# A two-layer decoder trunk on one core: pads in SBUF that move matmul operands to other offsets modulo 256 bytes, and the inverse norm spread by transposes in place of products

## The chip, the cores and the metric

The kernel runs on one core of one Trainium2 chip, in one launch. The metric is the device time of that core in microseconds, from runs of the whole kernel. TensorE (PE; its weight loads are shown apart, as PEld), VectorE (DVE), ScalarE (ACT), GpSimd (POOL) and SyncE (SP, which here only issues DMAs) are separate engines that meet at semaphores. Each of them works through its own instructions in the order in which they stand in the program.

## The reference

Two layers on a sequence of 256 positions with 1024 features, all in float32. Layer 0 mixes tokens with a gated linear recurrence (RG-LRU), layer 1 with sparse attention in three branches. A squared-ReLU MLP follows each, with an RMS norm ahead of every part and one at the end.

```python
def _rmsnorm(x, g):
    y = xf * lax.rsqrt(jnp.mean(xf * xf, axis=-1, keepdims=True) + RMS_EPS)
    return (y * g.astype(jnp.float32)).astype(x.dtype)

def _sq_relu_mlp(h, w_up, w_down):
    u = jax.nn.relu(h @ w_up)
    return (u * u) @ w_down

def reference(x, ...):
    for i in range(DEPTH):
        h = _rmsnorm(x, norm_mix[i])
        if i % N_MIXERS == 0:
            x = x + _rglru_mixer(h, ...)
        else:
            x = x + _nsa_mixer(h, ...)
        h = _rmsnorm(x, norm_ffn[i])
        x = x + _sq_relu_mlp(h, mlp_w_up[i], mlp_w_down[i])
    return _rmsnorm(x, norm_final)
```

`_rglru_mixer` is a projection to 2048 features, a causal convolution of width 4, two sigmoid gates from block-diagonal products, a scan over the sequence and a projection back. `_nsa_mixer` is a projection to queries, three pairs of keys and values and gates; a compressed branch whose softmax also scores blocks; a selected and a window branch; and a projection back.

## The kernel before

**Layout.** Activations lie transposed: 128 features on the partitions, 256 positions along the free axis, eight such chunks for 1024 features. Weights arrive in pieces of 128x1024 values by DMA (tile `raw`, 5 buffers). Every product of a weight piece is made in three matmuls so that it keeps float32's precision: a weight `w` is split into a rounded part `whi` (ACT, sometimes DVE) and the rest `wlo` (DVE), 7 buffers of each, and an activation into such a pair too. `mm3` (L313 to L315) then issues `whi` by the high part, `whi` by the low part, `wlo` by the high part, all into one PSUM bank. One such matmul has a stationary operand of 128x128 (a 512-byte stretch of `whi` or `wlo` in each partition), and a moving operand of 128x256 (1024 bytes in each partition).

**Moving operands.** `hhl` holds the pair of the normalised input, for the projections (`conv`, `branch`, `proj`, MLP up). `uhl` holds that of the squared ReLU, for MLP down. `xbh` and `xbl` hold that of the recurrence's output, for its output projection (`out`, 192 matmuls). `oh` and `ol` hold that of the attention's output. In attention, `kh` and `kl` are the moving operands of the scores (L1095, L1096, with the queries `sa` or `sb` stationary), `kc` that of the compressed scores (L1032), `pth` and `ptl` those of the product of probabilities and values (L1160, L1162, with `vhl` stationary), and `pc` that of the compressed branch (L1167, with `bhl` stationary). The recurrence's gates (L656) are plain float32 products with `gw` stationary and `xb` moving.

**Stages.** The recurrence, the attention and the lead into each MLP are written as tasks with due times, durations and dependencies; a planner (`Plan`) turns them into one order for each engine when the program is built. The two MLPs are plain loops: 32 up pieces and 32 down pieces each, 24 matmuls a piece. PE has work from the first pieces to the last in one stream. DVE and ACT prepare the weight pieces ahead of it.

**The norm.** The factor 1/sqrt(mean square) is applied after the projection, so the projections need not wait for it. Four times in the program (`Section.stats`) and once at its end these steps run: `square_sums` (L491) sums the squares of the features for 128 positions at a time, with a column of ones moving, which leaves the sums with the positions on the partitions; ACT takes the square root (L408) and DVE the reciprocal (L410) into `rcol`, 128x2; `spread` (L496) brings it back along the free axis, equal on all partitions; ACT copies that from PSUM to `rs`, called `rstd` in the profile (L412). DVE then multiplies projections by `rs` as it reads them from PSUM. At the end of the program the last step is left out: DVE multiplies `xg` by the PSUM bank itself (L1274) and the result goes out by DMA.

**Pools.** A pool of buffers gives each tile the next free bytes of every partition, in the order in which the tiles are named. A tile in its midst therefore sets where all the later ones of that pool start.

Of the kernel before, what the change touches and what calls it, by code (L numbers as in the profile page):

```python
# [12 lines left out]
F32 = mybir.dt.float32  # L13
# [6 lines left out]
P = 128  # L20
S = 256
# [203 lines left out]
def trunk_kernel(ctx: ExitStack, tc: tile.TileContext, x_in, vec_in, const_in, w2_in, wts, out):  # L225
    nc = tc.nc
    ctx.enter_context(tc.manual_schedule())
    pe, dve, act, pool = nc.tensor, nc.vector, nc.scalar, nc.gpsimd
# [9 lines left out]
    def bank(i):  # L238
        return psum.tile([P, 512], F32, name="bank%d" % i, tag="bank%d" % i)
# [88 lines left out]
    class Section:  # L328
# [73 lines left out]
        def stats(self, srcs, t):  # L402

            b6 = [("ps", 6)]
            st = self.bank(("stats", t), 6, lambda x: x)
            for j, (x, k) in enumerate(srcs):
                self.add("pe", 0.32, lambda e, j=j, x=x: square_sums(st(), x, j == 0, j == len(srcs) - 1), r=[k], w=b6, t=t)
            self.add("act", 0.15, lambda e: e.activation(rcol, st()[:, :2], AF.Sqrt, bias=epst, scale=1.0 / D), r=b6 + ["tab"],  # L408
                     w=["rcol"], t=t)
            self.add("dve", 0.08, lambda e: e.reciprocal(rcol, rcol), w=["rcol"], t=t)  # L410
            self.add("pe", 0.43, lambda e: spread(st()), r=["rcol", "cst"], w=b6, t=t)
            self.add("act", 0.26, lambda e: e.copy(rs, st()[:, S:]), r=b6, w=["rs"], t=t)  # L412
# [36 lines left out]
    ident = cst[:, C_ID:C_ID + P]  # L449
# [7 lines left out]
    rcol = spool.tile([P, 2], F32, name="rcol")  # L457
# [35 lines left out]
    def spread(st):  # L493

        for i in range(2):
            pe.matmul(st[:, S + i * P:S + (i + 1) * P], rcol[:, i:i + 1].to_broadcast([P, P]), ident, start=True, stop=True)  # L496

    def residual(z, m):
        dve.tensor_tensor(xt[:, m], xt[:, m], z, op=OP.add)  # L499
# [2 lines left out]
    with ExitStack() as ph:  # L502
        rg = ph.enter_context(tc.tile_pool(name="rg", bufs=1))
# [91 lines left out]
        small(lambda e: e.tensor_scalar(sp, sp, 4.0, None, op0=OP.mult), [], ["sp"])  # L595

        xb_b, r_b, i_b, y_b, t_b = (rg.tile([P, 8, S], F32, name=n) for n in ("xb", "r", "i", "y", "t"))
        xbh_b, xbl_b = (rg.tile([P, 8, S], F32R, name=n) for n in ("xbh", "xbl"))
        xb, r_t, i_t, y_t, t_t, xbh, xbl = ([x[:, m] for m in range(8)] for x in (xb_b, r_b, i_b, y_b, t_b, xbh_b, xbl_b))
        pair = lambda x, m: x[:, m // 2 * 2:m // 2 * 2 + 2]  # L600
# [185 lines left out]
    with ExitStack() as ph:  # L786
        at = ph.enter_context(tc.tile_pool(name="at", bufs=1))
# [14 lines left out]
        th, tl = many([P, S], F32R, "th", 2), many([P, S], F32R, "tl", 2)  # L802
        ptt = at.tile([P, NPT * 6 * P], F32, name="pt")
        pts = [ptt[:, i * 6 * P:(i + 1) * 6 * P] for i in range(NPT)]
        kh = at.tile([P, 4, 2 * S], F32R, name="kh")
        kl = at.tile([P, 4, 2 * S], F32R, name="kl")
        kc = at.tile([P, 4, 2, NCP], F32R, name="kc")
        osumt = at.tile([P, 2, S], F32, name="osum")
        osum = [osumt[:, i] for i in range(2)]
        identf = cst[:, C_ID:C_ID + P]  # L810
        zw = [at.tile([P, 8 * S], F32, name="zw" + n, tag=n) for n in ("oh", "ol")]
        ohl = {}

        def opart(n, i):

            if n not in ohl:
                ohl[n] = at.tile([P, 8 * S], F32R, name=n, tag=n)
            return ohl[n][:, i * S:(i + 1) * S]

        oh, ol = (lambda i, n=n: opart(n, i) for n in ("oh", "ol"))  # L820
        ptht, ptlt = (at.tile([P, NTH * 3 * P], F32R, name=n) for n in ("pth", "ptl"))
        pth, ptl = ([x[:, i * 3 * P:(i + 1) * 3 * P] for i in range(NTH)] for x in (ptht, ptlt))
        add("pool", 0.15, lambda e: e.memset(kc.bitcast(F32), 0.0), w=["kc0"], t=-9)
# [442 lines left out]
    st = bank(6)  # L1266
    mlp(1, to_final, up1, lambda: square_sums(st, acc, True, False))
    square_sums(st, sqs[1], False, True)
    act.activation(rcol, st[:, :2], AF.Sqrt, bias=epst, scale=1.0 / D)
    dve.reciprocal(rcol, rcol)  # L1270
    spread(st)

    for i, (a, n) in enumerate(((0, 1), (1, 1), (2, 2), (4, 2), (6, 1), (7, 1))):
# [113 lines left out]
```

## Time and profile before

| | us |
|---|---|
| median of 3 runs | 593.32 |
| lowest and highest run | 591.52, 593.86 |
| span of the profiled execution, first to last instruction | 588.7 |
| PE busy in that span | 572.6 |
| DVE busy | 421.5 |
| ACT busy | 356.5 |

The page gives the profiled execution by its span; a time of its own beside the span isn't given. The median of the runs lies 4.6 us above the span.

A row of the groups reads: line, engine, operation, output<-inputs, shapes, count, then the busy time in us and the mean time of one in ns, then the idle time of the engine ahead of them and what ended it. A matmul's time in such a row is from its start to its modelled end; the next one on PE starts well before that end. How fast PE goes through a row of matmuls is read from their starts, or from the number of them in a window. A plain float32 product of 128x128 operands is one instruction in the program and two records in the profile; a transpose is one.

### The profile page before, as it was taken

The page shows a single profiled execution, that of the slowest core. Times are in us where ns is not written, and L with a number is a line of the kernel's source. Part 1 is how long each engine was busy: PE and PEld are TensorE (multiplying, and loading weights), DVE is VectorE, ACT ScalarE, POOL GpSimd, SP SyncE. Part 2 cuts the span into 40 slices and gives each one's busy share as a digit, 9 for nine tenths or more (in the row PEclk, how much of TensorE's full clock was granted, in tenths as well). Part 3 has the DMA queues.
Part 4 walks back from the last instruction along what each step waited for, and adds up shares of the span by engine and source line. Part 5 has one row for each costly group of instructions (what it writes and reads, how often), then busy time and mean ns, then how long its engine had stood idle before and what let it go on. Part 6 is the DMA issues. An engine that isn't in the chain of part 4 may idle for free.

```text
span 588.7 us, 12309 instructions
## 1 busy us (share of the span) xinstructions
PE 572.6 (97%) x4798; PEld 559.1 (95%) x4798; DVE 421.5 (72%) x862; ACT 356.5 (61%) x711; POOL 75.2 (13%) x110
## 2 busy tenths in 40 slices
PE   7999999999999999999999999989999999999994
PEld 7999999999999999999989997879999999999994
DVE  6899997776766546547679999989876776464522
ACT  7699583766664325336367999996866564343410
POOL 2210000000001113125211532000000000132320
PEclk9999999999999999999999999999999999999998
DMA  8934665665666665657954641143776667466302
GB/s 285 386 119 136 208 221 183 216 206 183 192 201 197 210 205 175 210 188 228 232 197 144 180 128 52 37 125 99 238 201 199 188 206 239 158 183 228 126 2 72
DMA packets 32682, 105.74 MB, mean 180 GB/s; under 512 B 4832, under 2 KB 6496, under 8 KB 32624
## 3 DMA queue, kind: packets, MB, share of 16 engines
q1 hardware_dynamic: 30224, 100.70, 53.3%
q0 software_dynamic: 1824, 3.72, 2.5%
q8 instruction: 38, 0.62, 0.5%
q10 hardware_dynamic: 576, 0.53, 0.3%
q14 instruction: 20, 0.16, 0.1%
HBM read 99.23 MB, written 1.05 MB: 170 GB/s over the span
## 4 chain that ended last, share of the span: by engine, by line
PE 81%; ACT 8%; DVE 6%; issue 3%; DMA 1%; POOL 0%; SPq 0%; DVEq 0%; ACTq 0%; POOLq 0%
PE bank L315 25%; PE bank L313 25%; PE bank L314 25%; PE bank L656 2%; ACT pt L1105 2%; ACT pt L1124 2%; DVE wlo L318 1%; ACT pth L1138 1%; ACT whi L321 1%; PE bank L906 1%; DMA raw<-in_dram 1%; ACT osum L1171 1%; DVE ptl L1139 1%; DVE pt L1102 1%; DVE osum L1174 1%
## 5 line engine op out<-in xcount | busy, mean ns | idle before, releaser
L313 PE MATMUL bank<-hhl,whi 128*128 128x256 f32 x768 | 214.3, 279 | 1.6 <-DVE whi L321 1.6
L315 PE MATMUL bank<-hhl,wlo 128*128 128x256 f32 x768 | 212.7, 277 | 0.8 <-DVE wlo L318 0.8
L314 PE MATMUL bank<-hhl,whi 128*128 128x256 f32 x768 | 212.3, 276 | 0.0
L282 DVE TENSOR_TENSOR wlo<-raw,whi 128x1024 fp32r<-128x1024 f32 x118 | 147.3, 1269 | 2.7 <-ACT whi L273 2.7
L313 PEld LDWEIGHTS bank<-hhl,whi 128*128 128x128 f32 x768 | 144.2, 188 | 2.2 <-ACT whi L321 1.5
L315 PEld LDWEIGHTS bank<-hhl,wlo 128*128 128x128 f32 x768 | 144.2, 188 | 1.6 <-DVE wlo L318 1.4
L314 PEld LDWEIGHTS bank<-hhl,whi 128*128 128x128 f32 x768 | 144.4, 188 | 0.1
L313 PE MATMUL bank<-uhl,whi 128*128 128x256 f32 x512 | 141.4, 276 | 0.0
L315 PE MATMUL bank<-uhl,wlo 128*128 128x256 f32 x512 | 141.4, 276 | 0.0
L314 PE MATMUL bank<-uhl,whi 128*128 128x256 f32 x512 | 141.4, 276 | 0.0
L273 ACT CAST whi<-raw 128x1024 fp32r<-128x1024 f32 x119 | 120.9, 1039 | 23.7 <-issue 18.8
L314 PEld LDWEIGHTS bank<-uhl,whi 128*128 128x128 f32 x512 | 96.1, 188 | 0.0
L313 PEld LDWEIGHTS bank<-uhl,whi 128*128 128x128 f32 x512 | 96.1, 188 | 0.0
L315 PEld LDWEIGHTS bank<-uhl,wlo 128*128 128x128 f32 x512 | 96.1, 188 | 0.0
L318 DVE TENSOR_TENSOR wlo<-raw,whi 128x1024 fp32r<-128x1024 f32 (+3 forms) x72 | 76.0, 1073 | 2.6 <-ACT whi L321 2.6
L499 DVE TENSOR_TENSOR xt<-xt,bank 128x256 f32<-128x256 f32 x40 | 16.0, 417 | 85.6 <-PE bank L315 85.4
L321 ACT CAST whi<-raw 128x1024 fp32r<-128x1024 f32 (+2 forms) x65 | 61.5, 957 | 17.4 <-PE bank L314 9.5
L751 ACT ACTIVATE u<-t 128x256 f32<-128x256 f32 x64 | 26.7, 417 | 54.9 <-DVE t L746 54.9
L746 DVE SCALAR_TENSOR_TENSOR t<-bank,rstd 128x256 f32<-128x256 f32 x64 | 26.9, 423 | 42.5 <-PE bank L315 41.7
L469 POOL TENSOR_TENSOR acc<-xt 128x256 f32<-128x256 f32 x2 | 3.0, 1522 | 301.1 <-DVE xt L499 301.1
L1264 ACT ACTIVATE xg<-xt,vec 128x256 f32<-128x256 f32 x8 | 4.1, 510 | 48.0 <-DVE xt L499 48.0
L1105 ACT ACTIVATE pt<-pt,mx 128x256 f32<-128x256 f32 (+1 forms) x64 | 28.7, 452 | 3.4 <-DVE mx L1102 3.2
(201 smaller groups left out, 830.5 us busy)
## 6 DMA issues: line engine op xcount, KB each, us to landing
raw<-in_dram SPq DMA_DIRECT2D x175, 512.0 KB, 4.3
gw<-in_dram SPq DMA_DIRECT2D x4, 512.0 KB, 8.4
raw<-in_dram SPq DMA_DIRECT2D x6, 256.0 KB, 5.3
xt<-in_dram SPq DMA_DIRECT2D x4, 256.0 KB, 5.0
kh<-th POOLq DMA_DIRECT2D x16, 64.0 KB, 4.2
raw<-in_dram SPq DMA_DIRECT2D x2, 456.0 KB, 4.8
zwoh<-in_dram SPq DMA_DIRECT2D x1, 512.0 KB, 4.9
zwol<-in_dram SPq DMA_DIRECT2D x1, 512.0 KB, 6.2
```

The costliest lines, as they stand in the source:

```text
L273: (act.copy if eng is None else eng.tensor_copy)(hi_t[i % NSPL][:, :n], raw_t[i % NRAW][:, :n])
L282: (eng or dve).tensor_tensor(lo[:, :n], raw_t[i % NRAW][:, :n], hi[:, :n].bitcast(F32), op=OP.subtract)
L313: pe.matmul(ps, wh, xh, start=start, stop=False)
L314: pe.matmul(ps, wh, xl, start=False, stop=False)
L315: pe.matmul(ps, wl, xh, start=False, stop=stop)
L318: return lambda e: e.tensor_tensor(o, a, h.bitcast(F32), op=OP.subtract)
L321: return lambda e: (e.copy if e is act else e.tensor_copy)(o, a)
L499: dve.tensor_tensor(xt[:, m], xt[:, m], z, op=OP.add)
L656: e.matmul(z(), gw[b][:, o:o + P], xb[2 * b + k], start=k == 0, stop=k == 1)
L746: dve.scalar_tensor_tensor(t, z, 0.0, rs, op0=OP.max, op1=OP.mult)
L751: act.activation(u, t, AF.Square)
L1105: add("act", (0.39, 0.49)[qc], lambda e, row=row, j=j: e.activation(row, row, AF.Exp, bias=mx[:, j:j + 1], scale=-1.0, accum_out=sm[:, j:j ...
```

## The change

Two parts. The first puts four tiles that nothing reads or writes into the pools: 128 bytes ahead of `xbh` in the recurrence, and 64, 192 and 64 bytes at three places in the attention. The second makes `spread` issue two transposes of the broadcast `rcol`, where it issued two float32 products with the identity. The stationary operand (`rcol`, one column repeated 128 times) and the moving one (the 128x128 identity in `cst`) are the same in both forms, and so is what they write.

```diff
     def spread(st):
 
         for i in range(2):
-            pe.matmul(st[:, S + i * P:S + (i + 1) * P], rcol[:, i:i + 1].to_broadcast([P, P]), ident, start=True, stop=True)
+            pe.transpose(st[:, S + i * P:S + (i + 1) * P], rcol[:, i:i + 1].to_broadcast([P, P]), ident)
...
         xb_b, r_b, i_b, y_b, t_b = (rg.tile([P, 8, S], F32, name=n) for n in ("xb", "r", "i", "y", "t"))
+        rg.tile([P, 32], F32, name="rgap")
         xbh_b, xbl_b = (rg.tile([P, 8, S], F32R, name=n) for n in ("xbh", "xbl"))
...
         pts = [ptt[:, i * 6 * P:(i + 1) * 6 * P] for i in range(NPT)]
+        at.tile([P, 16], F32, name="gap0")
         kh = at.tile([P, 4, 2 * S], F32R, name="kh")
         kl = at.tile([P, 4, 2 * S], F32R, name="kl")
         kc = at.tile([P, 4, 2, NCP], F32R, name="kc")
...
+        at.tile([P, 48], F32, name="gap1")
         zw = [at.tile([P, 8 * S], F32, name="zw" + n, tag=n) for n in ("oh", "ol")]
...
+        at.tile([P, 16], F32, name="gap2")
         ptht, ptlt = (at.tile([P, NTH * 3 * P], F32R, name=n) for n in ("pth", "ptl"))
```

Where the operands of the matmuls start within a partition, modulo 256 bytes, in the built program:

| operand | before | after |
|---|---|---|
| `whi`, `wlo` (stationary in `mm3`) | 32 | 32 |
| `hhl`, `uhl` | 224 | 224 |
| `oh`, `ol` (and `zw`, which shares their bytes) | 224 | 224 (256 bytes further on) |
| `xbh`, `xbl` | 96 | 224 |
| `gw` (stationary) | 192 | 64 |
| `xb` (moving with `gw`) | 96 | 96 |
| `kh`, `kl`, `kc` | 224 | 32 |
| `sa`, `sb`, `vhl`, `bhl` (stationary in attention) | 96 | 96 |
| `pth`, `ptl` | 224 | 32 |
| `pc` | 32 | 96 |

Tiles that only DVE, ACT or POOL work on and that are named behind a pad move too (`xp`, `a2`, `osum`, `mx`, `sm`, `cs` and others).

No engine's instructions change their order, and none is added or removed but those of `spread`, which keep their places. The planner's durations are not touched.

## The prediction

> **What bounds the kernel now.** I read the page first: engines, slices, chain.
>
> ```profile
> PE 572.6 (97%) x4798; PEld 559.1 (95%) x4798; DVE 421.5 (72%) x862; ACT 356.5 (61%) x711; POOL 75.2 (13%) x110
> PEclk9999999999999999999999999999999999999998
> PE 81%; ACT 8%; DVE 6%; issue 3%; DMA 1%; POOL 0%; SPq 0%; DVEq 0%; ACTq 0%; POOLq 0%
> ```
>
> PE is busy for 97% of the span at full granted clock, and 81% of the chain that ended last is PE's. So a nanosecond on a matmul counts, unless PE then waits for something else. A mean time from start to modelled end doesn't give the pace; starts do. I therefore asked for windows of PE alone in which one form fills the whole stretch: the recurrence's output projection, then the two MLPs.
>
> ```profile
> 66.40:88.20 21.80, 21.80 (x187) 1.00 0.72 239
> 95.70:260.00 164.30, 164.30 (x1452) 1.00 0.63 202
> 412.60:575.80 163.20, 163.20 (x1443) 1.00 0.56 176
> ```
>
> After the stretch come busy time and, in brackets, the matmuls that touch it; about two of these started before it. All are 128x128 by 128x256. In the MLPs a start follows the last one after 164.30/1450 = 113.3 ns (the second: 163.20/1441 = 113.3). In the output projection it takes 21.80/185 = 117.8 ns. The same difference stands in the groups of these windows, as 280 ns against 276:
>
> ```profile
> L314 PE MATMUL bank<-xbl,whi 128*128 128x256 f32 x62 | 17.4, 280 | 0.0
> L314 PE MATMUL bank<-uhl,whi 128*128 128x256 f32 x245 | 67.6, 276 | 0.0
> ```
>
> PE waits in neither (0.0 idle), and the stationary operands lie at 32 modulo 256 in both. What differs is the moving one: 96 for `xbl`, 224 for `uhl`. So this trace has two paces, **113.3 and 117.8 ns**, 4.5 apart, and the offset goes with them. It isn't all, though. The chain that ended last, in order of time around the third norm:
>
> ```profile
> 266.79 0.11 PE bank L313
> 266.90 0.11 PE bank L314
> 267.13 0.11 PE bank L313
> 267.54 0.58 PE bank L491 x4
> 268.12 0.23 PE bank L313
> 268.34 0.12 PE bank L314
> 268.46 0.12 PE bank L315
> 268.58 0.12 PE bank L313
> ```
>
> With `hhl` at 224 throughout, PE drops from 0.11 us a matmul to 0.12 when the square sums (L491) come between. It stays there until the spread, and returns behind it, as the timeline of the second norm shows:
>
> ```profile
> 94.57 0.28 PE L314 MATMUL bank<-hhl,whi 128*128 128x256 f32 x1
> 94.69 0.28 PE L315 MATMUL bank<-hhl,wlo 128*128 128x256 f32 x1
> 94.80 0.61 PE L496 MATMUL bank<-cst,rcol 128*128 128x128 f32 x4
> 95.17 0.37 PE L313 MATMUL bank<-hhl,whi 128*128 128x256 f32 x1
> 95.37 0.28 PE L314 MATMUL bank<-hhl,whi 128*128 128x256 f32 x1
> 95.49 0.28 PE L315 MATMUL bank<-hhl,wlo 128*128 128x256 f32 x1
> 95.60 0.28 PE L313 MATMUL bank<-hhl,whi 128*128 128x256 f32 x1
> 95.72 0.28 PE L314 MATMUL bank<-hhl,whi 128*128 128x256 f32 x1
> ```
>
> So the pace can also be held by what came just before. Behind each of the four spreads in the program it is the quick one, and behind two of them it then holds for a whole MLP.
>
> **The change, part by part.** *Output projection.* `xbh` and `xbl` go from 96 to 224, with `whi` and `wlo` at 32: the pair of the MLP rows. 192 matmuls x 4.5 ns = **0.86 us**. PE doesn't wait in that stretch, and the projection's last residual starts the norm, so the end moves with it.
>
> *Spread.* Four records become two. In the rows above they take 95.17 - 94.80 = 0.37 us to the next matmul's start. Transposes of this form run in attention:
>
> ```profile
> 327.99 0.28 PE L315 MATMUL bank<-hhl,wlo 128*128 128x256 f32 x1
> 328.11 0.49 PE L1135 MATMUL bank<-cst,pt 128*128 128x128 f32 x3
> 328.36 0.37 PE L313 MATMUL bank<-hhl,whi 128*128 128x256 f32 x1
> 328.56 0.28 PE L314 MATMUL bank<-hhl,whi 128*128 128x256 f32 x1
> ```
>
> Three take 0.25 us to the next start. The last step is about 0.03 and the others 0.11, so two take 0.14 and a spread saves 0.23. At the first, second and fourth PE goes on without a wait, so it counts: 0.69. At the third it doesn't, for PE stands at 271.2 for a weight piece that hangs on ACT and DVE, not on the spread:
>
> ```profile
> 268.89 1.06 ACT whi L321
> 269.98 1.24 DVE wlo L318
> 271.26 0.38 PE bank L315
> ```
>
> The fifth stands in the tail, where nothing hides it:
>
> ```profile
> 581.39 0.17 DVE L1270 RECIPROCAL rcol<-rcol 128x2 f32<-128x2 f32 x1 [0.99 <-ACT rcol L1269]
> 581.62 0.71 PE L496 MATMUL bank<-cst,rcol 128*128 128x128 f32 x4 [0.55 <-DVE rcol L1270]
> 582.37 0.75 DVE L1274 TENSOR_TENSOR xg<-xg,bank 128x256 f32<-128x256 f32 x2 [0.80 <-PE bank L496]
> ```
>
> It gives 0.22, two steps of 0.11. Spread in all: **0.91 us**.
>
> *Attention's operands.* `kh`, `kl`, `pth` and `ptl` go from 224 to 32 with stationary operands at 96. That is the pair that `pc` and `bhl` have now:
>
> ```profile
> L1160 PE MATMUL bank<-pth,vhl 128*128 128x256 f32 x16 | 4.5, 280 | 0.0
> L1167 PE MATMUL bank<-pc,bhl 128*128 128x256 f32 x16 | 3.2, 283 | 0.0
> L656 PE MATMUL bank<-xb,gw 128*128 128x256 f32 x64 | 14.1, 379 | 0.0
> ```
>
> Neither is at 276. Against a gain, the new pair stands at 283. For one, 224 less 32 and 32 less 96 are both 192 modulo 256, and `pc` runs only two at a time, which may not be enough to settle. Bounds for these 128 matmuls: nothing, or 128 x 4.5 = 0.58 us; the other way 128 x 3 = 0.38 lost (283 against 280). I take 0.2 gained, near the middle, since part of it lies beside waits for ACT and DVE. `pc` (16 matmuls) and `kc` (32 columns) are too few or too short to count. `gw` moves to 64: its matmuls take 379 ns for the two passes, long enough to cover a load, so I take nothing, with 64 x 4.5 = 0.29 either way. DVE's and ACT's tiles that move keep their cost: nothing in the groups of these engines separates equal shapes by offset.
>
> *Sum:* 0.86 + 0.91 + 0.2 = 1.97 us. The profiled execution would span 588.7 - 2.0 = 586.7; with the 4.6 us by which the runs' median lies above the span, **591.3 us**, 0.3% less. Neither part changes what any engine issues elsewhere, so no DMA starts for another reason, and SP's and POOL's queues are untouched.
>
> One rule speaks against the pads. The Trainium skill, "TensorE: Matmul & The Clock Gate", section "Step-by-step: what each phase is for", has TensorE read its moving and its stationary operand through two independent ports, so that the next load takes nothing from the running matmul. By that alone, offsets wouldn't matter and the sum would be the spread's 0.9 us. This trace disagrees as far as it goes: 117.8 against 113.3 ns in one form.
>
> **The rivals.** *1. Transposes leave PE in the slow pace (slower).* What sets the pace behind an interruption the views don't tell. Behind square sums it is the slow one all five times that `mm3` follows, behind the product spread the quick one all four times. Transposes are in between. Windows of the matmuls behind them, in attention:
>
> ```profile
> L314 PE MATMUL bank<-hhl,whi 128*128 128x256 f32 x5 | 1.4, 281 | 0.0
> L314 PE MATMUL bank<-hhl,whi 128*128 128x256 f32 x8 | 2.2, 277 | 0.0
> ```
>
> The first is the stretch 319.2 to 320.7, the second 328.8 to 331.0. By starts in the timeline, of 14 places where `mm3` with an operand at 224 follows transposes, 11 reach the quick pace and 3 stay slow. If the second spread ends slow, nothing in MLP 0 breaks the stretch: 1450 matmuls x 4.5 = 6.5 us. The fourth does the same to MLP 1: 1441 x 4.5 = 6.5 us. Both: 591.3 + 13.0 = **604.3**; one: 597.8. It decides as soon as a slow stretch outlasts some 440 matmuls (1.97/0.0045). For it: both spreads are entered alike, from square sums and twelve slow matmuls, so a bad entry would hit both; the three slow places show that transposes can do it. Against: 11 of 14, and of those entered at a slow pace with no wait inside, 328.11 comes out quick.
>
> *2. The offset isn't the cause.* The pace of the output projection then has another reason, the pads give nothing, and only the spread's 0.9 us is left: 592.4. Against it, the two MLPs, `oh` and `hhl` are all quick at 224, while all three operands of the projection's `mm3` are slow at 96.
>
> *3. The transposes leave the clock.* The Trainium skill, same page, section "Part 4: PE-mode transpose", says that transposes don't count as busy for the clock gate. By it PE could be throttled behind them. The granted clock in the slices above is full through attention, with its 104 transposes, so no time is put to it.
>
> **How the numbers follow.** The forecast, quick pace kept: 0.55, with its own range 590.0 to 592.6 (bounds above: 0.58 gained or 0.38 lost in attention, 0.29 for `gw`, and some tenths between executions). Both MLPs slow: 0.30, more than 3/14, since one of the slow places is, as the spreads are, entered from slow `hhl` matmuls (320.99). One MLP slow: 0.08. Pads without effect: 0.07. To leave out no more than 2 in 10 the range has to reach rival 1: **590.0 to 605.2**. About 0.5% (3 us) is what a measurement of this kernel can tell from no change. Faster by more needs 3.0 us where I find 2.0: 0.09. Within it: the rest of the forecast and rival 2, 0.53. Slower: 0.38.
>
> **What would show it.** Output projection: 276 ns in place of 280 and 113.3 by starts. Spread: two records and about 0.14 us to the next start. MLPs: windows of 1450 matmuls stay near 164.3 us; at 170.8 rival 1 holds, and `uhl` rows read 281. Attention: `pth` and `kl` rows at 276 in place of 280. I would be wrong in the mechanism if `xbl` stays at 280, and in the main risk if the pace behind a spread isn't that of the whole MLP.

## The result, and the profile after

The changed kernel takes **597.58 us**, the median of nine executions; the kernel before takes 593.32 in nine beside them. The ratio is 1.0073, with a 95% interval of 1.0044 to 1.0102: slower, where 0.3% less was forecast. (The ratios here are the record's own; where a kernel's times fall into groups some us apart, they aren't the quotient of the medians.) Seven of the nine lie between 597.2 and 599.3; one took 592.6 and one 601.1.

The page of the changed kernel, engines, clock and chain:

```profile
PE 580.2 (97%) x4788; PEld 566.8 (95%) x4788; DVE 421.8 (71%) x862; ACT 356.8 (60%) x711; POOL 74.9 (13%) x110
PEclk9999999999999999999999999999999999999998
PE 79%; ACT 9%; DVE 5%; issue 3%; DMA 2%; POOL 1%; SPq 1%; DVEq 0%; ACTq 0%; POOLq 0%
```

PE has ten records fewer and is busy 7.6 us longer, at full clock; DVE, ACT and POOL are as before. Windows of PE alone say where, as in the prediction; the first is the output projection, then MLP 0 and MLP 1:

```profile
62.50:92.00 29.50, 29.50 (x253) 1.00 0.64 210
96.50:260.00 163.50, 163.50 (x1445) 1.00 0.63 202
413.50:576.50 163.00, 163.00 (x1386) 1.00 0.56 177
```

With two matmuls off for the start, as before: 117.5 ns a start in the projection, 113.3 in MLP 0, **117.8 in MLP 1**. Two rows of the timeline tie MLP 1 down, the fourth spread and the square sums behind the MLP, in the kernel before and then in the changed one:

```profile
411.64 0.61 PE L496 MATMUL bank<-cst,rcol 128*128 128x128 f32 x4
575.99 0.50 PE L491 MATMUL bank<-ones,acc 128*128 128x1 f32 x4
```

```profile
412.62 0.38 PE L496 MATMUL bank<-cst,rcol 128*128 128x128 f32 x2
583.15 0.50 PE L491 MATMUL bank<-ones,acc 128*128 128x1 f32 x4
```

Up to the fourth spread the changed kernel is 0.98 us late (412.62 - 411.64). From there to the square sums it takes 170.53 us against 164.35, so 6.18 more. The rest takes 595.5 - 583.15 = 12.35 us against 588.7 - 575.99 = 12.71, so 0.36 less. The sum is the 6.8 us by which the span grew. Nearly all of it is what rival 1 of the prediction puts to one MLP, 6.5 us.

Groups of the changed kernel that answer to those of the prediction:

```profile
L314 PE MATMUL bank<-xbl,whi 128*128 128x256 f32 x64 | 18.0, 281 | 0.0
L1164 PE MATMUL bank<-pth,vhl 128*128 128x256 f32 x16 | 4.5, 281 | 0.0
L496 PE MATMUL bank<-cst,rcol 128*128 128x128 f32 x10 | 2.0, 277 | 0.6 <-DVE rcol L1274 0.6
```

`xbl` stays at 281, though it now stands at 224. `pth` stays too. Only the spread did what was said.

### The profile page after: what moved, and what is told of

Its sections match the earlier page's. It is cut to its first block, busy times and chain, and to the rows that moved or that the text cites. A ratio compares the mean times of both kernels' runs of the same rounds, so it can differ in the third digit from the quotient of the medians.

```text
span 595.5 us, 12289 instructions
## 1 busy us (share of the span) xinstructions
PE 580.2 (97%) x4788; PEld 566.8 (95%) x4788; DVE 421.8 (71%) x862; ACT 356.8 (60%) x711; POOL 74.9 (13%) x110
## 4 chain that ended last, share of the span: by engine, by line
PE 79%; ACT 9%; DVE 5%; issue 3%; DMA 2%; POOL 1%; SPq 1%; DVEq 0%; ACTq 0%; POOLq 0%
PE bank L313 25%; PE bank L315 25%; PE bank L314 24%; ACT pt L1109 3%; PE bank L657 2%; ACT pt L1128 2%; ACT pth L1142 1%; ACT whi L321 1%; DMA kl<-tl 1%; DVE wlo L318 1%; PE bank L910 1%; ACT osum L1175 1%; SPq L346 1%; DMA vec<-in_dram 1%; DVE osum L1178 1%
## 5 line engine op out<-in xcount | busy, mean ns | idle before, releaser
L313 PE MATMUL bank<-hhl,whi 128*128 128x256 f32 x768 | 216.5, 282 | 0.8 <-DVE whi L321 0.8
L315 PE MATMUL bank<-hhl,wlo 128*128 128x256 f32 x768 | 214.9, 280 | 0.5 <-DVE wlo L318 0.5
L314 PE MATMUL bank<-hhl,whi 128*128 128x256 f32 x768 | 214.5, 279 | 0.0
```

The source lines that it names most:

```text
L313: pe.matmul(ps, wh, xh, start=start, stop=False)
L314: pe.matmul(ps, wh, xl, start=False, stop=False)
L315: pe.matmul(ps, wl, xh, start=False, stop=stop)
```

## The experiments

Three questions: which part of the change costs the time; what decides the pace; and whether the gain can be had without the loss. "Quick" is 113.3 ns from start to start in `mm3`, "slow" 117.8.

### The two parts apart

The kernel before with the transposes alone (first line), and with the pads alone (the four pads and the product spread):

```diff
-            pe.matmul(st[:, S + i * P:S + (i + 1) * P], rcol[:, i:i + 1].to_broadcast([P, P]), ident, start=True, stop=True)
+            pe.transpose(st[:, S + i * P:S + (i + 1) * P], rcol[:, i:i + 1].to_broadcast([P, P]), ident)
```

> The transposes alone, no pads. Theory CARRY (mm3 has two stable paces, 113.3 and 117.8 ns a matmul; what stands just ahead of a stretch decides which one, and the stretch keeps it): the changed kernel's loss in MLP 1 comes with the transposes, so here too the stretch behind the fourth spread (1440 matmuls, 163 us before) should take about 6.4 us more in most executions, and the output projection stays at 117.8 as before; time 593.3 - 0.9 + 6.4 = 598.8 us, or 592.4 in an execution where no spread ends slow. Rival OFFSET (the loss comes from the moved operands): MLP 1 stays at 113.3 and the time is 592.4 us, 0.9 below before.

> The pads alone, with the spread by products. CARRY: both MLPs stay at 113.3 ns, since products stand ahead of them. The slow stretch from the gates' end (44.3 us) to the second norm (93.7 us) stays slow, because it begins behind the gate matmuls, whose stationary operand gw has moved: 187 hhl matmuls lose 0.8 us, and the output projection at 224 gains nothing; time about 594.1 us. Rival OFFSET (an operand at 224 with a weight at 32 is quick by itself): xbl at 276 ns and 113.3 by starts, 0.86 gained, about 592.3 us.

The transposes alone take 603.41 us (median of 10; ratio 1.013, 1.0082 to 1.0177): four executions at 598 to 600, six at 603 to 607. The pads alone take 603.9 (median of 4: 600.2, 600.9, 606.9, 607.5; ratio 1.0169, 1.0095 to 1.0243). So **each part by itself loses**, by the medians more than both together. The second was a surprise: its spread is the product form, which I had taken to leave quick always. Windows of both MLPs, first of the kernel with transposes, then of that with pads:

```profile
96.50:260.00 163.50, 163.50 (x1390) 1.00 0.59 197
419.50:582.50 163.00, 163.00 (x1387) 1.00 0.55 177
```

```profile
97.00:260.50 163.50, 163.50 (x1391) 1.00 0.59 197
422.50:585.50 163.00, 163.00 (x1441) 1.00 0.55 176
```

With transposes both MLPs are slow; with pads it is MLP 0. The chain of the kernel with pads, in order of time, shows how MLP 0 got there:

```profile
94.03 0.12 PE bank L315
94.15 0.34 PE bank L491 x4
94.49 0.23 PE bank L313
94.72 0.11 PE bank L314
...
95.85 0.11 PE bank L315
95.97 0.44 PE bank L496 x4
96.41 0.12 PE bank L313
96.53 0.12 PE bank L314
```

PE comes slow (0.12) to the square sums, leaves them quick (0.11), and the product spread leads it from quick into slow. In the kernel before it was the other way round: quick into the square sums, slow out, and the same spread led from slow into quick. So the pace behind the spread isn't a property of the spread alone: it depends on the pace in which PE comes.

### Which offsets can be quick

The kernel before with `whi` and `wlo` in steps of 32 bytes (seven buffers at seven offsets), `hhl` and `uhl` at 224.

```diff
-    hi_t = [wpool.tile([P, WMAX], F32R, name="whi%d" % i) for i in range(NSPL)]
-    lo_t = [wpool.tile([P, WMAX], F32R, name="wlo%d" % i) for i in range(NSPL)]
+    hi_t, lo_t = [], []
+    for x, n in ((hi_t, "whi"), (lo_t, "wlo")):
+        for i in range(NSPL):
+            x.append(wpool.tile([P, WMAX], F32R, name="%s%d" % (n, i)))
+            wpool.tile([P, 16 if i == NSPL - 1 else 8], F32, name="%sgap%d" % (n, i))
```

> Kernel before, with pads between the weight buffers: whi0 to whi6 and wlo0 to wlo6 start at 32, 64, 96, 128, 160, 192 and 224 modulo 256, while hhl and uhl stay at 224, so that the difference moving less stationary is 192, 160, 128, 96, 64, 32 and 0. The starts of each 24 matmuls give the pace by difference. If 192 alone can be quick, as the rows of before suggest, six of seven pieces in the MLPs run at about 117.8 and the time rises by up to 6/7 x 2900 x 4.5 ns = 11 us, to some 604 us. If the pace is only carried (CARRY without any part for the offset), all pieces of an MLP run alike. If other differences are quick as well, they show 113.3 or less.

One execution, 609.8 us, more than the 604 expected at most. PE in 160 us of MLP 0:

```profile
100.00:260.00 160.00, 160.00 (x1354) 1.00 0.59 196
```

That is 118.3 ns on average, with no wait. By the starts in the timeline, for whole pieces of 24 matmuls, some 20 for each difference (offset of the moving operand less that of the stationary one, modulo 256; the profile leaves buffer numbers out, so the offsets are those of the built program, matmul by matmul):

| difference | 0 | 32 | 64 | 96 | 128 | 160 | 192 |
|---|---|---|---|---|---|---|---|
| mean ns, start to start | 119.7 | 117.8 | 117.8 | 119.9 | 118.7 | 117.3 | 117.8, once 113.4 |

So the offsets matter: the spread is from 117.3 to 119.9 in one form, and of the whole pieces only one was quick, at 192. It begins right behind the gates (30.5 us); the others follow another piece, at the difference 0, and stay slow. Shorter rows are not in the table, and two of them were quick at another difference, 64: 18 matmuls ahead of the second square sums, and 12 ahead of the third spread. The first of the two:

```profile
92.97 0.28 PE L316 MATMUL bank<-hhl,whi 128*128 128x256 f32 x1
93.09 0.28 PE L317 MATMUL bank<-hhl,whi 128*128 128x256 f32 x1
...
94.90 0.28 PE L318 MATMUL bank<-hhl,wlo 128*128 128x256 f32 x1
95.01 0.50 PE L494 MATMUL bank<-ones,acc 128*128 128x1 f32 x4
```

From 92.97 to 95.01 that is 113.3 ns for each of the 18. The difference 224 occurs only in rows of six, of the output projection, none of them quick. So 192 isn't the only difference that can be quick. In long rows the two still part. The output projection of the other profiles stands at 64 or, with the pads, at 192. At 64 it was slow in eight of eight, two of which came to it quick; at 192 it kept the pace in which PE came in seven of seven, three of them quick. Neither the offset alone nor the history alone gives the pace: **192 permits the quick pace for a long row, and what ran before decides whether it is taken.**

A change of the operands can itself turn the pace. In the kernel before, `hhl` comes back behind the slow projection at 89.5 us, with nothing between, and is quick at once; with transposes alone it stays slow there.

The Trainium skill, "TensorE: Matmul & The Clock Gate", section "Step-by-step: what each phase is for", has the two operands read through independent ports; by it the seven columns would be equal, and they differ by 2.6 ns.

### Kinds of interruption

The kernel before with one of seven interruptions, in turn, ahead of nearly every MLP piece.

```diff
+        for i, x in enumerate({"A": "pp", "B": "tt", "D": "tp", "E": "pt", "F": "t", "G": "ttt"}[kind]):
+            (prod if x == "p" else tr)(i)
...
                     wh, wl = get("up%d" % layer, m)
+                    probe()
```

`p` is the spread's product, `t` its transpose, `C` two products of one column, like the square sums; they write a bank that is not read.

> Kernel before, with a short interruption on PE ahead of each weight piece of the MLPs, into a PSUM bank that nothing reads, in seven kinds by turns: two products as in the spread; two transposes; two one-column products as in the square sums; transpose then product; product then transpose; one transpose; three transposes. 24 mm3 matmuls follow each. Under CARRY the pace of these 24 goes by the kind ahead of them: products as the last thing give 113.3, one-column products give 117.8, transposes last give both. Rival: the pace behind doesn't go by the kind, and the slow MLP 1 of the changed kernel has another cause. The time itself rises by about 120 interruptions of 0.15 to 0.5 us and says nothing.

One execution, 638.4 us. The outcome repeated with the cycle: two products, entered quick, left slow 18 times of 18; transpose then product, entered slow, left quick 17 of 17; product then transpose, entered quick, quick 17 of 17; two transposes, entered slow, slow 18 of 18; one transpose, entered quick, slow each time; three transposes, entered slow, quick 17 of 17; the one-column pair, entered slow, slow 17 of 18. In this fixed cycle each kind has one entry only, so what kind and entry do apart stayed open. From here on I took as theory that kind and entry together decide.

### `gw` held, and `gw` alone

The pads put `gw` from 192 to 64. The pads with one more of 128 bytes that holds `gw` at 192, and the kernel before with that pad alone:

```diff
+        rg.tile([P, 32], F32, name="rgap2")
         gw = many([P, 1024], F32, "gw", 4)
```

> All the pads, the product spread, and one more pad of 128 bytes ahead of gw, so that gw stays at 192 as before. CARRY (the pace of a stretch is what the interruption ahead of it leaves; the offset only says which pairs can be quick at all): if gw's offset is what made the gates' exit slow, the output projection now starts quick and stays so at 224: x187 window at 113.3 ns a start in place of 117.8, 0.86 us less than with the pads alone; the spreads of the MLPs are the same products in the same surroundings as before, so both MLPs quick and about 592.4 us. OFFSET (the moving operand's offset alone sets the pace): output projection 113.3, and MLPs quick in every run, 592.4. PHASE (what an interruption leaves hangs on the exact time at which it begins, so any shift upstream can change it): the MLPs come out either way, 592.4, 598.9 or 605.4, with no bearing on gw.

> The kernel before with one pad of 128 bytes ahead of gw alone (gw from 192 to 64; what is named behind gw in that pool moves with it). CARRY: the stretch behind the gates (187 projection matmuls with hhl, quick before) turns slow, 187 x 4.5 ns = 0.84 us, and the MLPs stay as before: 594.2 us. OFFSET: no matmul of mm3 changes its pair, so 593.3. PHASE: MLPs either way, 594.2, 600.7 or 607.2 in different runs.

`gw` alone: 592.8 us (median of 9; ratio 0.9988, 0.9942 to 1.0035), no difference that can be told (one execution took 600.45). Yet its profile has the slow stretch behind the gates. 15 us of it, in the kernel before and in this one:

```profile
45.00:60.00 15.00, 15.00 (x134) 1.00 0.37 111
```

```profile
45.20:60.20 15.00, 15.00 (x130) 1.00 0.38 117
```

With `gw` held, four executions of nine lie at 591.2 to 592.1, four at 597.9 to 599.6 and one at 605.6 (ratio 1.001, 0.994 to 1.0081). In its profile (591.5 us) the projection is quick, as CARRY had it; that both MLPs would be quick in every run, as it also had, is missed. What the executions near 598 are, two more profiled executions of the same kernel show:

> The kernel with the pads, gw held at 192 and the product spread once more, for a look at one of its executions near 598 (5 of 9 were). SWITCH: its stretches are one chain from the first weight pieces to the second norm (nothing between changes the pairing of offsets any more), so an execution near 598 is slow already at the first pieces (10 to 18 us), the square sums turn it to quick, the first spread to slow, the projection is slow, the second square sums leave quick and the second spread leads MLP 0 into the slow pace. An execution near 591.5 starts quick. If instead the first pieces are quick and MLP 0 slow, or MLP 1 is the slow one, the chain isn't the reason.

> The same kernel again: the same two cases, so that one of each may be seen.

By luck, one took 591.18 us and the other 600.82. Projection and MLP 0, of the first and then of the second:

```profile
62.50:92.00 29.50, 29.50 (x263) 1.00 0.65 213
95.70:259.20 163.50, 163.50 (x1446) 1.00 0.61 202
```

```profile
62.50:92.00 29.50, 29.50 (x252) 1.00 0.66 212
96.50:260.00 163.50, 163.50 (x1391) 1.00 0.60 197
```

The chain is as expected: a slow projection, square sums that leave quick, a product spread that leads into slow. Its beginning isn't where I expected it. The first pieces are quick in both. The slow pace begins behind a short wait, just ahead of the projection: a step of 0.16 us at 61.24 us, as DVE's `wlo` of that piece ends at 61.12. The quick execution has the same step at 61.41 and stays quick. So a wait for data, too, can let PE out in either pace, and the next 1800 matmuls depend on it. Nine of the fifteen profiles that the count below goes over come quick to this wait: five leave it quick, the kernel before among them, and four slow.

### Other spreads

The kernel before with a transpose and then a product, and with three transposes:

```diff
+        pe.transpose(st[:, S:S + P], rcol[:, 0:1].to_broadcast([P, P]), ident)
+        pe.matmul(st[:, S + P:S + 2 * P], rcol[:, 1:2].to_broadcast([P, P]), ident, start=True, stop=True)
```

> The kernel before with a spread of one transpose and then one product. In the run with interruptions ahead of each piece this kind left the quick pace 17 of 17 times after a slow entry, and the spreads are entered slow. CARRY with kind and entry deciding: both MLPs quick in every run, 593.3 less 0.1 for each of five spreads = 592.9 us. PHASE: the MLPs come out either way from run to run, 592.9, 599.4 or 605.9.

> The kernel before with a spread of three transposes (the first block is written twice). After a slow entry this kind left the quick pace 17 of 17 times in the run with interruptions. CARRY with kind and entry deciding: both MLPs quick in every run, 593.3 less 0.12 for each of five spreads = 592.7 us. PHASE: the MLPs come out either way from run to run, 592.7, 599.2 or 605.7. If the number of transposes doesn't matter (transposes always leave the slow pace): 603.4 as with two.

592.86 us (10 executions, 591.3 to 594.6; ratio 0.9974, 0.9929 to 1.002) and 593.07 (10, 591.5 to 595.7; 0.9975, 0.9932 to 1.0018). Neither has an execution near 598, where 8 of the 30 of the kernel before in this comparison were above 598. In both profiles both MLPs are quick. With three transposes, though, the first spread, entered slow, left slow at 21 us, against the 17 of 17; transpose then product left quick each time.

### One more interruption, two more, and two transposes

If two products turn the pace over, one more pair in the midst of an MLP must cost it, and a second one must give it back.

```diff
+    def again():
+        pb = bank(7)
+        for i in range(2):
+            pe.matmul(pb[:, i * P:(i + 1) * P], rcol[:, i:i + 1].to_broadcast([P, P]), ident, start=True, stop=True)
...
                     wh, wl = get("up%d" % layer, m)
+                    if m in (8,):
+                        again()
```

> The kernel before, and in each MLP one more pair of the spread's products, written to a bank that is not read, ahead of the ninth up piece, some 190 matmuls behind the spread and 1344 before the next norm. SWITCH: PE enters the pair quick, so it leaves slow, and nothing turns it back: 592.7 + 2 x 1344 x 4.5 ns + 2 x 0.37 us = 605.5 us, 117.8 ns a start behind the pair in both MLPs. CHANCE: either pace, 593.4, 599.5 or 605.5 from run to run. If products always leave quick, as the prediction had it: 593.4.

> As the one with one more pair, and a second such pair two pieces (48 matmuls) later. SWITCH: slow for 48 matmuls, then quick again: 592.7 + 2 x 48 x 4.5 ns + 4 x 0.37 us = 594.6 us, that is 11 us faster than with one pair, though it does more. CHANCE: either pace, 594.2 to 605.5. If products always leave quick: 594.2, slower than with one pair by 0.7.

One more pair: 604.29 us (3 executions, 603.9 to 605.6; ratio 1.0189, 1.0136 to 1.0241). Two more: **594.3** (9, 593.5 to 596.0; 1.0027, 1.0002 to 1.0052). The kernel that does more is 10 us faster. In its profile the 48 matmuls between the pairs of an MLP are slow, and the rest is quick again.

Then the same place with two transposes in `again`:

> As the one with one more pair of products ahead of the ninth up piece, with two transposes in place of the products. KEEP (two transposes leave PE in the pace in which it came, so the loss of the changed kernel is that they no longer turn the slow pace that the square sums leave): PE comes quick and stays quick, 592.3 + 2 x 0.14 = 592.6 us. TOSLOW (two transposes leave the slow pace whatever was before): 592.3 + 2 x 1344 x 4.5 ns = 604.4 us, as with one more pair of products.

592.46 us (9, 591.7 to 594.2; ratio 0.9974, 0.9936 to 1.0013). MLP 0 behind the added pair, of products and then of transposes, with the same number of matmuls in each window:

```profile
113.00:273.00 160.00, 160.00 (x1361) 1.00 0.57 188
```

```profile
113.30:267.30 154.00, 154.00 (x1361) 1.00 0.59 195
```

117.7 against 113.3 ns. Two transposes that PE enters quick leave it quick: they don't lead into the slow pace, they leave the quick one as it is.

### The pads with another spread

The two sets of pads, with `gw` held or not, and transpose then product as the spread:

> The pads, gw held at 192, and a spread of a transpose and then a product. SWITCH (what leaves an interruption hangs on the pace in which PE enters it and on its kind: two products turn slow to quick and quick to slow, transpose and product lead from slow to quick, square sums entered quick leave slow): the output projection is entered quick and stays so at 224, the square sums leave slow, the spreads leave quick, both MLPs 113.3 in every run: 592.7 - 0.86 for the projection - 5 x 0.11 for a transpose in place of a product = 591.3 us, no run near 598. CHANCE (the pace behind each interruption is drawn anew by the exact time): as with the products, about half of the runs near 598.

> The changed kernel with a spread of a transpose and then a product in place of two transposes; gw stays at 64, as changed. The stretch from the gates to the second square sums is then slow (419 matmuls at 117.8). SWITCH: square sums entered slow leave either pace; from a slow entry the spread leaves quick; from a quick entry it was never seen. If it leaves quick from both: both MLPs quick in every run, 592.7 + 187 x 4.5 ns for the stretch behind the gates - 0.55 = 593.0 us. If it turns the pace over, as products do: MLP 0 slow in many runs, near 599.8. CHANCE: either, in both MLPs.

With `gw` held: **591.32 us** (12 executions, 589.4 to 592.7, none near 598, where five of nine lay there or above with the same offsets and products) against 592.28 for the kernel before; ratio 0.9973, 0.995 to 0.9996. It is the fastest of all. With `gw` at 64, as changed: 593.1 (10; 1.0007, 0.998 to 1.0033); its second spread was entered quick, and left quick. The fastest one's windows, projection and both MLPs, and its `xbl`:

```profile
62.50:92.00 29.50, 29.50 (x262) 1.00 0.66 213
95.70:259.20 163.50, 163.50 (x1445) 1.00 0.64 203
413.30:576.30 163.00, 163.00 (x1440) 1.00 0.56 176
```

```profile
L314 PE MATMUL bank<-xbl,whi 128*128 128x256 f32 x64 | 17.7, 276 | 0.0
```

All three are quick (113.5, 113.3, 113.4 ns), and `xbl` is at the 276 that the prediction asked for.

### The count over all profiles

Spreads, added pairs, square sums and gates with ten `mm3` matmuls ahead and eleven behind and no wait in either, counted by their starts in fifteen profiles (all but those with moved `whi` and with seven kinds):

| interruption | quick to quick | quick to slow | slow to quick | slow to slow |
|---|---|---|---|---|
| two products (spread and `again`) | 0 | 7 | 26 | 0 |
| transpose, then product | 1 | 0 | 8 | 0 |
| two transposes (spread and `again`) | 3 | 0 | 2 | 3 |
| three transposes | 1 | 0 | 1 | 1 |
| square sums | 6 | 50 | 11 | 8 |
| gates with `gw` at 192 (two stretches a profile) | 18 | 0 | 0 | 4 |
| gates with `gw` at 64 (two stretches a profile) | 0 | 4 | 0 | 4 |

Two products turned the pace over in 33 of 33. Transpose then product left quick in 9 of 9. For the others kind and entry don't settle it. Of the slow entries to the square sums, the nine at the second norm part by what ran ahead: the four with the projection at the difference 192 (the pads) leave quick, the five with it at 64 leave slow. So PE carries more than the pace that the starts show; what, the traces don't tell.

## Why the prediction was wrong, point by point

**Output projection, 0.86 us: not had.** The pair came to 224 over 32 and stayed slow (117.5 ns). What failed here is the term for `gw`: "I take nothing". Its own matmuls do take what they took (379 ns in both profiles; that is one record, and a product is two), but the price lay behind them: with `gw` at 64 they lead PE from quick to slow, and 224 then holds the slow pace from there through the whole projection. That also slowed the 187 `hhl` matmuls ahead of it, quick before: 187 x 4.5 ns = 0.84 us. By the timeline, from the gates to the second square sums the changed kernel takes 0.77 us more (44.02 to 93.67, against 44.07 to 92.95). With `gw` held, the 0.86 us comes when PE enters quick (113.5 ns, 276), in three profiles of four. So the size was right and its condition was missed.

**Spread, 0.91 us: right.** In the row of 412.62 two transposes take 0.14 us to the next `mm3` (412.76), 0.36 for the products (411.64 to 412.00): 0.22 less, and as much at the other three spreads. At the third PE then waits for `wlo`, as said. The tail is 0.36 us shorter where 0.22 was said; 22 matmuls behind the last square sums are quick there, which adds 22 x 4.5 ns = 0.10.

**Attention, 0.2 us: not had.** `pth` went from 280 to 281, `kl` with `sa` from 279 to 281. The new pair has the difference 192 too, but runs only a few matmuls at a time; whether it could be quick in a long row isn't shown. From the end of PE's wait behind the third spread to the first `oh` matmul attention takes 124.46 us (271.73 to 396.19) against 123.94 (271.26 to 395.20), so 0.52 more. This and the 0.77 above, less some 0.3 at the first two norms, are the 0.98 us by which the fourth spread is late. The pads needn't be the reason: the same stretch takes 123.9 to 126.5 us in the profiles without the attention's pads and 124.5 to 127.1 in those with them.

**Quick pace kept, 0.55: this is the step that failed, and it cost 6.2 of the 6.8 us.** The prediction read four quick exits of four as "behind the product spread the quick one", and 11 of 14 places in attention as the odds of transposes. Both were taken as properties of the interruption. But all four spreads are entered slow, from the square sums, and two products turn slow to quick. The four of four were one case seen four times. And none of the 14 places has two transposes; they have three, five or six. In the run with seven kinds three led from slow to quick 17 times of 17, two not once in 18. Two transposes don't turn the pace over as two products do: entered slow they stayed slow in three places of five (and in those 18). The changed kernel, at the second spread and then at the fourth:

```profile
95.15 0.28 PE L313 MATMUL bank<-hhl,whi 128*128 128x256 f32 x1
95.26 0.28 PE L314 MATMUL bank<-hhl,whi 128*128 128x256 f32 x1
95.37 0.28 PE L315 MATMUL bank<-hhl,wlo 128*128 128x256 f32 x1
95.49 0.38 PE L496 MATMUL bank<-cst,rcol 128*128 128x128 f32 x2
...
96.53 0.28 PE L314 MATMUL bank<-hhl,whi 128*128 128x256 f32 x1
96.64 0.28 PE L315 MATMUL bank<-hhl,wlo 128*128 128x256 f32 x1
96.75 0.28 PE L313 MATMUL bank<-hhl,whi 128*128 128x256 f32 x1
```

```profile
412.27 0.28 PE L313 MATMUL bank<-hhl,whi 128*128 128x256 f32 x1
412.39 0.28 PE L314 MATMUL bank<-hhl,whi 128*128 128x256 f32 x1
412.51 0.28 PE L315 MATMUL bank<-hhl,wlo 128*128 128x256 f32 x1
412.62 0.38 PE L496 MATMUL bank<-cst,rcol 128*128 128x128 f32 x2
...
413.55 0.28 PE L313 MATMUL bank<-hhl,whi 128*128 128x256 f32 x1
413.67 0.28 PE L314 MATMUL bank<-hhl,whi 128*128 128x256 f32 x1
413.79 0.28 PE L315 MATMUL bank<-hhl,wlo 128*128 128x256 f32 x1
```

The `mm3` steps are 0.11 us ahead of the first spread, and 0.11 again a microsecond behind it (four slow ones lie between); they are 0.12 ahead of the second and stay 0.12 behind it, for the whole MLP (1446 matmuls to the square sums).

**Rival 1 had mechanism and price right, and one argument wrong.** One slow MLP was put at 6.5 us and cost 6.18, with the spread's 0.22 taken off. That its time, 597.8, lies so near the measured 597.6 is partly luck: its sum rests on the 1.06 us of the projection and attention, which weren't had, and on 4.6 us between span and median. By spans it gives 586.7 + 6.5 = 593.2, and 595.5 was measured. "A bad entry would hit both" fails because the entries aren't alike: ahead of MLP 0 the square sums, entered slow behind the pads' projection, left quick, so the transposes had nothing to turn. Two losses of the change cancel there. Without the pads (transposes alone) MLP 0 is lost as well; without the transposes (pads alone) the products turn that quick entry into a slow MLP 0.

**Span and median.** The 4.6 us between them was 1.8 in the changed kernel's own profiled execution (597.3 over 595.5 us), so the profiled execution of before was likely one of the lower ones. No step hangs on it.

**Rivals 2 and 3 fall.** The offset is a condition of the quick pace in a long row (the projection at 64 and at 192, above), and each part of the change alone costs time. The clock is granted in full in every window shown.

**Open.** How one matmul hands the pace to the next isn't shown; nor why two transposes left quick at the first spread, twice, and slow behind the others. Of the kernel before no execution near 598 was profiled, so that it loses an MLP in the same way is an inference from the times. Which one isn't known either: in the five profiles with the product spread and the projection at 64, the second spread was entered slow and left quick each time, whichever pace PE brought to the norm.

## What to carry to other kernels

Where a long row of matmuls can run at two paces, find out what led into each: read the steps from start to start on both sides of every interruption, and ask of an edit not only what the interruption costs but in which pace it leaves PE for the next thousand. A pattern that holds each time in one trace may hold because each time was entered alike, so look for a case with another entry before it becomes a rule. And a pad moves everything named behind it: what it was meant for was right here, and the tile it moved by the way (`gw`) undid it.

## What the runs showed of the hardware that was not expected

- A row of 128x128 by 128x256 matmuls, PE never waiting and the clock full, with operands at 224 over 32 keeps 113.3 or 117.8 ns for as long as nothing comes between: 1518 matmuls in one stretch. An interruption of 0.14 to 0.36 us sets it for the next 170 us.
- The pace goes with the difference of the operands' offsets modulo 256 bytes: whole pieces took 117.3 to 119.9 ns at six differences, and 117.8 or 113.4 at 192. Rows of 18 and 12 matmuls were quick at 64 too.
- Extra work can save time: a second pair of products in each MLP, 0.7 us in all, took 604.3 us to 594.3.
